# Partial sums of two middle chunks moved from one addition to a copy and an addition, with one weight buffer fewer

## The chip, the core and the metric

The kernel runs on one core of one Trainium2 chip. The core's engines are TensorE (PE: matmuls; PEld is its weight loads), VectorE (DVE), ScalarE (ACT), GpSimd (POOL) and SyncE (SP), which here only issues transfers (DMA). Each engine works through its own queue in order; semaphores tie the queues together. SBUF is the working memory, 128 partitions wide; PSUM is the memory that matmuls write to, eight banks of 128 x 512 float32. The metric is the time of one execution in microseconds, the median of the runs shown.

## What is computed

The reference is one layer of an encoder block over 256 tokens of width 2048. What the change touches is its first product, the combined input projection of the normalised and modulated tokens:

```python
mod = cond @ w_ada[l] + b_ada[l]
shift1, scale1, gate1, shift2, scale2, gate2 = jnp.split(mod, N_ADA, axis=-1)
h = modulate(rms_norm(x, norm_mix[l]), shift1, scale1)
proj = h @ w_in[l]
qa, ka, va, qi, ki, wi, qb, fb, ib, gb, g_a, g_b = split_columns(proj, IN_WIDTHS)
...
x = x + gate1[:, None, :] * (mixed @ w_out[l])
```

Behind it come an attention over selected keys, a gated recurrence, an output projection and a retrieval over 16384 experts. All products are float32, done as three products each: a matrix is split into a high part and a low rest, and high times high, high times low and low times high are added.

## The kernel before

**Phase 1, the projection sets.** 6144 of the projection's columns are computed in the loop `for c, ks in enumerate(CHUNKS)` as three sets `s` of 2048 columns, of which each fills the eight PSUM banks (16 column blocks of 256 tokens). The 16 k-tiles of 128 input features come in four chunks of 2, 3, 5 and 6. For each chunk and set, TensorE goes over the chunk's k-tiles, 48 matmuls each (a step; 48 steps in all), and adds them up in the eight banks. Then the banks are emptied into SBUF, and the next set uses them. In the first chunk the banks are copied, in turn by ScalarE and VectorE (L455, L457). In the three later chunks VectorE adds each bank to what is in SBUF (`nc.vector.tensor_add(d, d, p)`, L459). `into` tells the places: `dsa`, `qk`, `qkr`, `sgb`. In the first and the second set one bank goes to two places, so there are 26 pieces in a chunk: 22 of 128 x 512 and 4 of 128 x 256.

**The h1 tiles.** The k-tiles of h are made while the loop runs. `h1_tile(n)` needs two sums over 2048 products of the conditioning vector with a row of `w_ada` (VectorE, `ada_dot`, L186, tile `ada`), then GpSimd multiplies a tile of x by the root mean square (L240), ScalarE makes its high part (L242) and VectorE the modulated tile and the low part (L243, L244).

**The weights.** Class `Feed` loads weights in units of 128 x 1024 (512 KB), two for a step. `raw` (L76) issues a transfer on SP into the next of the `raw` buffers, which are used in turn: three of pool `raws` and two of pool `more`. `_split` makes the high part `hi` on ScalarE (L90) and the low part `lo` on VectorE, or on GpSimd for every third unit (L94, `pool_every = 3`, during phase 1's first part). There are three `hi` and three `lo` buffers; up to two units are split ahead. A `raw` buffer is free again when its `lo` is done. `ada_rest` takes `raw` buffers in the same turn for the other rows of `w_ada`, which one VectorE product consumes (L186, tile `raw`).

**Where the pools end.** `more` lives until the whole first phase ends (L874): sets, attention, recurrence, the gates, the projections `w_up`, and `w_out`. After that the feed has the three buffers of `raws` alone.

**Order.** The engines' queues are laid out by a scheduler when the program is built; `pin` keeps some instructions in the order of the program. The loop that empties the banks stands in the program behind the matmuls of its set.

Of the kernel before, what the change touches and what calls it, by code (L numbers as in the profile page):

```python
# [8 lines left out]
F32 = mybir.dt.float32  # L9
# [5 lines left out]
AF = mybir.ActivationFunctionType  # L15
# [5 lines left out]
P = 128  # L21
# [83 lines left out]
def build(tc, a):  # L105
    nc = tc.nc
    root = ExitStack()
    const = root.enter_context(tc.tile_pool(name="const", bufs=1))
    raws = root.enter_context(tc.tile_pool(name="raws", bufs=3))
# [6 lines left out]
    def bank(name="bank"):  # L116
        return psum.tile([P, 512], F32, tag="bank", name=name)
# [4 lines left out]
    feed = Feed(nc, [raws], his, los, ahead=2)  # L122
# [14 lines left out]

    p1 = ExitStack()
    k16 = p1.enter_context(tc.tile_pool(name="k16", bufs=7))
    more = p1.enter_context(tc.tile_pool(name="more", bufs=2))  # L140
    feed.raw_pools = [raws, more, raws, more, raws]

    def big(dt=F32, name="big"):
        return k16.tile([P, 4096], dt, tag="k16", name=name)

    ctx1 = ExitStack()


    small = ctx1.enter_context(tc.tile_pool(name="small", bufs=1))
# [14 lines left out]
    def ada_load(g):  # L164
        t = big(name="ada").rearrange("p (s k) -> p s k", s=2)
        for sec in range(2):
            tc.keep_in_program_order(nc.sync.dma_start(t[:, sec, :], a["w_ada1"][g, sec]))
        ada_tiles[g] = t

    feed.pin = tc.keep_in_program_order  # L170
    CHUNKS = (range(0, 2), range(2, 5), range(5, 10), range(10, 16))
# [254 lines left out]
    for c, ks in enumerate(CHUNKS):  # L426
        for s in range(3):
            banks = [bank(f"set{s}_{b}") for b in range(8)]
            for k in ks:
                if step in loads:  # L430
                    ada_load(loads[step])
                if feed.todo:
                    feed.load()
                    feed.load()
                if step == 40:
                    feed.pin = None
                units = [feed.next(), feed.next()]
                if step in makes:
                    h1_tile(makes[step])
                for b in range(16):  # L440
                    whi, wlo = units[b // 8]
                    out = banks[b // 2][:, (b % 2) * T:(b % 2 + 1) * T]
                    i = products(out, whi, wlo, (b % 8) * 128, hh[:, k, :], hl[:, k, :],
                                 k == ks[0] and b % 2 == 0, k == ks[-1],
                                 after=prev if k == ks[0] and b % 2 == 1 else None)
                    prev = i
                step += 1
                if c == len(CHUNKS) - 1 and step >= 36:
                    ada_bg.run(1700)
            for i, (ps, dst) in enumerate(zip(banks, into[s])):  # L450
                parts = [(dst, ps)] if not isinstance(dst, tuple) else [
                    (d, ps[:, z * T:(z + 1) * T]) for z, d in enumerate(dst)]
                for d, p in parts:
                    if c == 0 and i % 2:
                        nc.vector.tensor_copy(d, p)  # L455
                    elif c == 0:
                        nc.scalar.activation(d, p, AF.Copy)  # L457
                    else:
                        nc.vector.tensor_add(d, d, p)  # L459

# [105 lines left out]
    for c in range(2):  # L566
        ps = s_block(hh, hl, *W_A)
# [191 lines left out]
    for c in range(2):  # L759
        ps = s_block(hh, hl, *W_A)  # L760
# [793 lines left out]
```

## Time and profile before

| | us |
|---|---|
| median of 3 runs | 2158.49 |
| lowest and highest run | 2154.59, 2158.61 |
| the profiled execution | 2151.07 |
| its span, first to last instruction | 2149.2 |

| engine | busy, us | share of the span |
|---|---|---|
| PE | 2035.7 | 95% |
| PEld | 1841.5 | 86% |
| DVE | 1644.7 | 77% |
| ACT | 1068.9 | 50% |
| POOL | 1025.7 | 48% |

The first matmul of the sets starts at 29 us, the last ends at 355 us; the four chunks begin at about 29, 74.4, 141.2 and 237.8 us. Busy time is an average over stages; a stage is read by its own stretch, and by the waits that end last in it. A wait stands as "who waits <- for whom".

### The profile page before, as it was taken

How to read it: one execution, taken by the hardware profiler on the slowest of the kernel's cores; microseconds unless marked ns; L12 is line 12 of the kernel's file. 1: busy time of each engine (PE TensorE's matmuls, PEld its weight loads, DVE VectorE, ACT ScalarE, POOL GpSimd, SP SyncE). 2: the span in 40 equal slices, each digit the busy share in tenths (PEclk: the TensorE clock that was granted, in tenths of full speed). 3: DMA queues.
4: the chain of work that ended last, by engine and by line, in shares of the span. 5: the costliest groups of instructions: out<-in, count | busy, mean ns of one | idle time of the engine just before them, and what ended most of it. 6: DMA issues, size and time to landing. Idle time of an engine off the chain costs nothing. (4 is left out here: it accounts for less than half of the span.)

```text
span 2149.2 us, 34359 instructions
## 1 busy us (share of the span) xinstructions
PE 2035.7 (95%) x12916; PEld 1841.5 (86%) x12916; DVE 1644.7 (77%) x2538; ACT 1068.9 (50%) x1559; POOL 1025.7 (48%) x663
## 2 busy tenths in 40 slices
PE   6989999999999999999999999998999989999996
PEld 6988998779999999899888888887888778886885
DVE  7899888878675888887999666687558776765687
ACT  3433334455645445444666555543554445654575
POOL 3333422224420001218777688777871026777763
PEclk8999999999999999999999999999999999999998
DMA  6878778676677899857777898899879979999994
GB/s 252 310 267 317 258 254 288 207 239 210 214 236 263 312 334 326 310 176 183 180 181 186 231 262 257 249 324 291 223 212 360 319 261 334 282 261 268 386 382 178
DMA packets 208832, 568.65 MB, mean 265 GB/s; under 512 B 57585, under 2 KB 89489, under 8 KB 191633
## 3 DMA queue, kind: packets, MB, share of 16 engines
q1 hardware_dynamic: 147248, 441.38, 59.5%
q0 software_dynamic: 58928, 123.94, 21.5%
q8 instruction: 103, 1.69, 0.3%
q10 hardware_dynamic: 2482, 1.07, 0.2%
q14 instruction: 71, 0.58, 0.1%
HBM read 544.95 MB, written 38.06 MB: 271 GB/s over the span
## 5 line engine op out<-in xcount | busy, mean ns | idle before, releaser
L90 ACT ACTIVATE hi<-raw 128x1024 fp32r<-128x1024 f32 x550 | 580.9, 1058 | 686.0 <-PE ps_w L120 270.6
L94 DVE TENSOR_TENSOR lo<-raw,hi 128x1024 fp32r<-128x1024 f32 x506 | 652.5, 1292 | 256.0 <-ACT hi L90 254.3
L120 PE MATMUL ps_w<-h,hi 128*128 128x512 f32 (+1 forms) x2560 | 811.9, 373 | 12.7 <-ACT hi L90 7.4
L120 PE MATMUL ps_w<-h,lo 128*128 128x256 f32 x2304 | 649.5, 282 | 10.5 <-DVE lo L94 10.5
L921 POOL DMA_INDIRECT gtab<-gate,addr x256 | 508.7, 1987 | 174.9 <-issue 70.9
L120 PEld LDWEIGHTS ps_w<-h,hi 128*128 128x128 f32 x2560 | 465.0, 189 | 100.1 <-ACT hi L90 9.2
L120 PEld LDWEIGHTS ps_w<-h,lo 128*128 128x128 f32 x2304 | 437.0, 190 | 17.4 <-DVE lo L94 16.6
L120 PE MATMUL out<-vh,ap 128*128 128x512 f32 x1008 | 313.3, 391 | 2.8 <-ACT vh L225 2.8
L226 DVE TENSOR_TENSOR vl<-v,vh 128x1024 fp32r<-128x1024 f32 x190 | 224.6, 1224 | 72.7 <-ACT vh L225 70.7
L94 POOL TENSOR_TENSOR lo<-raw,hi 128x1024 fp32r<-128x1024 f32 x44 | 117.6, 2673 | 294.1 <-ACT hi L90 294.1
L120 PEld LDWEIGHTS out<-vh,ap 128*128 128x128 f32 x1008 | 189.5, 188 | 44.4 <-ACT vh L225 5.3
L225 ACT ACTIVATE vh<-v 128x1024 fp32r<-128x1024 f32 x190 | 189.8, 1047 | 72.4 <-DMA v<-w_v,index 67.7
L120 PE MATMUL set<-h1hi,hi 128*128 128x256 f32 x768 | 212.3, 291 | 13.5 <-ACT h1hi L242 7.1
L120 PE MATMUL set<-h1hi,lo 128*128 128x256 f32 x768 | 198.5, 293 | 22.1 <-DVE lo L94 18.9
L120 PE MATMUL set<-h1lo,hi 128*128 128x256 f32 x768 | 212.8, 288 | 0.9 <-DVE h1lo L244 0.9
L120 PE MATMUL out<-vl,ap 128*128 128x512 f32 x504 | 197.6, 392 | 4.9 <-DVE vl L226 4.9
L186 DVE SCALAR_TENSOR_TENSOR raw<-raw,cond 128x1024 f32<-128x1024 f32 x96 | 134.2, 1404 | 49.6 <-DMA raw<-w_ada 45.9
L120 PEld LDWEIGHTS set<-h1hi,hi 128*128 128x128 f32 x768 | 150.1, 198 | 16.6 <-ACT h1hi L242 7.3
L120 PEld LDWEIGHTS set<-h1hi,lo 128*128 128x128 f32 x768 | 141.2, 199 | 26.6 <-DVE lo L94 23.1
L120 PE MATMUL ps_w<-h1hi,hi 128*128 128x256 f32 x528 | 150.8, 286 | 3.0 <-ACT hi L90 3.0
L120 PE MATMUL ps_w<-h1hi,lo 128*128 128x256 f32 x528 | 150.3, 285 | 1.9 <-DVE lo L94 1.9
L120 PEld LDWEIGHTS set<-h1lo,hi 128*128 128x128 f32 x768 | 150.9, 197 | 1.2 <-DVE h1lo L244 1.2
(356 smaller groups left out, 3196.6 us busy)
## 6 DMA issues: line engine op xcount, KB each, us to landing
raw<-w_u SPq DMA_DIRECT2D x256, 512.0 KB, 4.4
raw<-w_sets SPq DMA_DIRECT2D x96, 512.0 KB, 5.4
raw<-w_ada SPq DMA_DIRECT2D x96, 512.0 KB, 5.1
raw<-w_t SPq DMA_DIRECT2D x66, 512.0 KB, 4.6
ada<-w_ada SPq DMA_DIRECT2D x32, 1024.0 KB, 8.3
raw<-w_s SPq DMA_DIRECT2D x32, 512.0 KB, 4.6
gtab<-zeros_d SPq DMA_DIRECT2D x32, 512.0 KB, 5.5
raw<-w_up SPq DMA_DIRECT2D x32, 512.0 KB, 4.7
```

Of the source, the lines that this page charges most:

```text
L90: self.nc.scalar.activation(hi, raw, AF.Copy)
L94: i = eng.tensor_sub(lo, raw, hi.bitcast(F32))
L120: return nc.tensor.matmul(out, lhsT, rhs, start=start, stop=stop, skip_group_check=True)
L186: return nc.vector.scalar_tensor_tensor(w, w, 1.0, cond[:, k0:k0 + n], op0=ALU.mult, op1=ALU.mult, accum_out=col)
L225: nc.scalar.activation(hi, v, AF.Copy)
L226: (lo_eng or nc.vector).tensor_sub(lo, v, hi.bitcast(F32))
L921: return nc.gpsimd.indirect_dma_start(out=gtab[tt].rearrange("p (x o) -> (p x) o", o=1), out_offset=bass.IndirectOffsetOnAxis(ap=addr[:, t ...
```

## The change

In the second and the third chunk a bank is no longer added to SBUF by VectorE in one instruction. ScalarE copies the bank into a tile `part`, and GpSimd adds `part` to the place in SBUF. There are two `part` buffers of 128 x 512 (2 KB of a partition each), in a pool that lives as long as the other small tiles of phase 1. Their 4 KB are those of one `raw` buffer: pool `more` has one instead of two, and the feed turns through four buffers instead of five. First and last chunk are emptied as before.

```diff
     p1 = ExitStack()
     k16 = p1.enter_context(tc.tile_pool(name="k16", bufs=7))
-    more = p1.enter_context(tc.tile_pool(name="more", bufs=2))
-    feed.raw_pools = [raws, more, raws, more, raws]
+    more = p1.enter_context(tc.tile_pool(name="more", bufs=1))
+    feed.raw_pools = [raws, more, raws, raws]
...
     ctx1 = ExitStack()
+    parts = ctx1.enter_context(tc.tile_pool(name="parts", bufs=2))
...
             for i, (ps, dst) in enumerate(zip(banks, into[s])):
-                parts = [(dst, ps)] if not isinstance(dst, tuple) else [
+                pieces = [(dst, ps)] if not isinstance(dst, tuple) else [
                     (d, ps[:, z * T:(z + 1) * T]) for z, d in enumerate(dst)]
-                for d, p in parts:
+                for d, p in pieces:
                     if c == 0 and i % 2:
                         nc.vector.tensor_copy(d, p)
                     elif c == 0:
                         nc.scalar.activation(d, p, AF.Copy)
+                    elif c < len(CHUNKS) - 1:
+                        part = parts.tile([P, 512], F32, name="part")[:, 0:p.shape[1]]
+                        nc.scalar.activation(part, p, AF.Copy)
+                        nc.gpsimd.tensor_add(d, d, part)
                     else:
                         nc.vector.tensor_add(d, d, p)
```

The lines of the changed kernel have numbers one higher from here on, and five higher below the loop: L90 and L94 stay, L186 is L187, L240 is L241, L242 to L244 are L243 to L245; the copies are L461, the additions L462.

GpSimd's queue in the second chunk, before: low parts of weights (`lo`, L94) and tiles of x (L240) alone.

```order
L240 TENSOR_TENSOR x<-x,rs 128x256
L94 TENSOR_TENSOR lo<-raw,hi 128x1024 x2
L240 TENSOR_TENSOR x<-x,rs 128x256
L94 TENSOR_TENSOR lo<-raw,hi 128x1024 x2
L240 TENSOR_TENSOR x<-x,rs 128x256
```

The same place of the changed kernel, from the end of that chunk's first set on:

```order
L462 TENSOR_TENSOR dsa<-dsa,part 128x512 x4
L462 TENSOR_TENSOR qk<-qk,part 128x512 x2
L94 TENSOR_TENSOR lo<-raw,hi 128x1024
L241 TENSOR_TENSOR x<-x,rs 128x256
L462 TENSOR_TENSOR qk<-qk,part 128x512
L462 TENSOR_TENSOR qk<-qk,part 128x256
L462 TENSOR_TENSOR dsa<-dsa,part 128x256
L462 TENSOR_TENSOR qk<-qk,part 128x512 x3
L94 TENSOR_TENSOR lo<-raw,hi 128x1024
```

Six additions now stand ahead of a `lo` and a tile of x, and three or four more before the next set's.

ScalarE's queue at the same set's end, before: high parts of weights (`hi`, L90) and of h1 (L242).

```order
L90 ACTIVATE hi<-raw 128x1024 x5
L242 ACTIVATE h1hi<-x,mod 128x256
L90 ACTIVATE hi<-raw 128x1024 x3
L242 ACTIVATE h1hi<-x,mod 128x256
L90 ACTIVATE hi<-raw 128x1024 x4
```

And in the changed kernel, where `set_3_665` is bank 3 of the set that ends and `set_0_888` bank 0 of the next:

```order
L461 ACTIVATE part<-set_3_665 128x512
L90 ACTIVATE hi<-raw 128x1024
L461 ACTIVATE part<-set_4_666 128x512
L461 ACTIVATE part<-set_5_667 128x512
L90 ACTIVATE hi<-raw 128x1024
L243 ACTIVATE h1hi<-x,mod 128x256
L461 ACTIVATE part<-set_6_668 128x512
L461 ACTIVATE part<-set_7_669 128x256
L90 ACTIVATE hi<-raw 128x1024
L461 ACTIVATE part<-set_7_669 128x256
```

One or two copies, of which each waits for a free `part`, now stand ahead of each `hi`.

VectorE's queue at the end of that set, before:

```order
L459 TENSOR_TENSOR qk<-qk,set_5_664 128x512
L459 TENSOR_TENSOR qk<-qk,set_6_665 128x512
L459 TENSOR_TENSOR qk<-qk,set_7_666 128x256
L459 TENSOR_TENSOR dsa<-dsa,set_7_666 128x256
L186 SCALAR_TENSOR_TENSOR ada,dots<-ada,cond 128x2048
L235 TENSOR_SCALAR mod<-dots,bada,cols 128x1
L94 TENSOR_TENSOR lo<-raw,hi 128x1024
```

And in the changed kernel in the same chunk:

```order
L245 TENSOR_TENSOR h1lo<-x,h1hi 128x256
L94 TENSOR_TENSOR lo<-raw,hi 128x1024
L187 SCALAR_TENSOR_TENSOR ada,dots<-ada,cond 128x2048 x2
L236 TENSOR_SCALAR mod<-dots,bada,cols 128x1
L94 TENSOR_TENSOR lo<-raw,hi 128x1024
L238 TENSOR_SCALAR mod<-dots,bada 128x1
```

The additions are gone; `lo` and the `ada` products stand next to each other, the two products of a tile in a row.

## Rows read from the trace of the kernel before

**Rows 1.** Busy time by stretch; columns in the first line.
```profile
core 0: us, PE busy (x) PEld busy (x) DVE busy (x) ACT busy (x) POOL busy (x), PEclk, DMA share, GB/s
74.40:141.20 66.80, 57.45 (x435) 56.02 (x434) 62.89 (x71) 21.70 (x23) 25.07 (x11) 0.92 0.74 278
141.20:237.80 96.60, 88.52 (x723) 86.83 (x722) 92.07 (x92) 35.08 (x36) 39.28 (x16) 1.00 0.78 290
...
690.00:903.00 213.00, 210.40 (x1751) 209.81 (x1750) 179.06 (x254) 96.83 (x128) 15.94 (x13) 1.00 0.90 319
```

**Rows 2.** PE's waits, 74.4 to 237.8 us: total us, times, longest.
```profile
PE set L120 <- DVE lo L94: 12.8, 9, 3.5
PE set L120 <- DVE qk L459: 3.6, 3, 1.8
```

**Rows 3.** Groups, 74.4 to 237.8 us: count, busy us, mean ns, idle before.
```profile
L186 DVE SCALAR_TENSOR_TENSOR ada<-ada,cond 128x2048 f32<-128x2048 f32 x22 | 62.3, 2832 | 0.0
L94 DVE TENSOR_TENSOR lo<-raw,hi 128x1024 fp32r<-128x1024 f32 x32 | 54.6, 1707 | 2.7 <-ACT hi L90 2.7
L90 ACT ACTIVATE hi<-raw 128x1024 fp32r<-128x1024 f32 x48 | 50.8, 1059 | 81.6 <-PE set L120 76.2 <-issue 5.4
L94 POOL TENSOR_TENSOR lo<-raw,hi 128x1024 fp32r<-128x1024 f32 x16 | 46.2, 2887 | 97.3 <-ACT hi L90 97.3
L240 POOL TENSOR_TENSOR x<-x,rs 128x256 f32<-128x256 f32 x11 | 19.4, 1762 | 0.0
```

**Rows 4.** Line 459, whole span: duration ns min/median/max, first and last start.
```profile
L459 DVE TENSOR_TENSOR qk<-qk,set x27: 405/674/689, 96.5 to 319.3; 128x512 f32<-128x512 f32 x21, 128x256 f32<-128x256 f32 x6
```

**Rows 5.** VectorE's timeline, 91 to 114 us: start us, us, instruction.
```profile
97.08 1.21 DVE L94 TENSOR_TENSOR lo<-raw,hi 128x1024 fp32r<-128x1024 f32 x1
...
107.61 2.28 DVE L186 SCALAR_TENSOR_TENSOR ada<-ada,cond 128x2048 f32<-128x2048 f32 x1
...
110.16 3.42 DVE L94 TENSOR_TENSOR lo<-raw,hi 128x1024 fp32r<-128x1024 f32 x1
```

**Rows 6.** GpSimd's timeline, 91 to 170 us.
```profile
109.81 2.69 POOL L94 TENSOR_TENSOR lo<-raw,hi 128x1024 fp32r<-128x1024 f32 x1 [3.53 <-ACT hi L90]
...
166.18 2.40 POOL L94 TENSOR_TENSOR lo<-raw,hi 128x1024 fp32r<-128x1024 f32 x1 [8.59 <-ACT hi L90]
168.53 0.74 POOL L240 TENSOR_TENSOR x<-x,rs 128x256 f32<-128x256 f32 x1
```

**Rows 7.** GpSimd's timeline, 505 to 516 us, in the recurrence.
```profile
508.42 1.30 POOL L678 TENSOR_TENSOR zt<-zt,qkr 128x512 f32<-128x512 f32 x1 [1.51 <-ACT zt L674]
509.68 1.31 POOL L679 TENSOR_TENSOR zt<-zt,qkr 128x512 f32<-128x512 f32 x1
510.94 2.28 POOL L681 TENSOR_TENSOR zt<-zt,qkr 128x512 f32<-128x512 f32 x1
```

**Rows 8.** Busy time and granted clock, two stretches; columns as in the first group.
```profile
130.00:135.00 5.00, 1.46 (x13) 1.25 (x11) 5.00 (x7) 0.48 (x1) 3.22 (x2) 0.84 0.85 354
133.00:140.00 7.00, 5.09 (x24) 5.09 (x25) 6.75 (x11) 1.66 (x2) 0.78 (x1) 0.53 0.74 236
```

**Rows 9.** Line 76's loads, 279 to 346 us: count, issue ns; time to landing.
```profile
L76 SPq DMA_DIRECT2D raw<-w_sets x20: 327/328/441, 279.8 to 336.6; - x20
L76 SPq DMA_DIRECT2D raw<-w_ada x17: 327/328/387, 279.5 to 344.9; - x17
...
DMA to landing us min/median/max: 3.7/5.4/7.1
```

**Rows 10.** Line 76's loads, 803 to 886 us.
```profile
L76 SPq DMA_DIRECT2D raw<-w_out x29: 327/328/328, 804.5 to 886.0; - x29
L76 SPq DMA_DIRECT2D raw<-w_ada x23: 327/328/328, 803.1 to 884.3; - x23
...
DMA to landing us min/median/max: 3.8/5.0/6.1
```

**Rows 11.** SP's waits, 803 to 886 us: total us, times, longest.
```profile
SPq L76 <- DVE lo L94: 34.4, 25, 2.4
```

## The prediction

> **What bounds the kernel now.** I first read the stretches of the page's timeline by chunk. The second and third chunk of k-tiles run from 74.4 to 237.8 us, 163.4 us. TensorE issues 24 steps of 48 matmuls there, 1152 in all; where nothing holds it, it starts 1751 in 213 us, 0.1216 us each [rows 1], so 140 us would do and some 23 us are lost. The PE waits say to whom: VectorE's `lo` 12.8 us, VectorE's additions out of PSUM 3.6 us [rows 2]. VectorE is busy 155 of the 163.4 us, ScalarE 57, GpSimd 64 [rows 1]. So VectorE bounds this stretch, and the change takes work from it: at first sight a gain of up to 23 us.
>
> The question is why VectorE is so full. In the groups of instructions its `ada` products take 2832 ns in the mean where one undisturbed takes 2.28 us, and its `lo` 1707 ns where one takes 1.21 [rows 3, 5]. The timeline of the two engines shows why: GpSimd's `lo` runs from 109.81 to 112.50, and VectorE's `lo`, begun at 110.16, takes 3.42 us, that is the rest of GpSimd's instruction and then its own 1.2 [rows 5, 6]. An operation with two SBUF inputs on one engine and one on the other exclude each other. The additions from PSUM are different: the 27 into qk, over the whole stage, lie between 405 and 689 ns (the three other destinations, 51 more, alike) [rows 4]. They never waited. The change takes away the VectorE work that runs beside GpSimd, and gives GpSimd work that doesn't run beside VectorE.
>
> The Trainium skill, page "SBUF — State Buffer", section "Who interferes with whom", says the same as a rule: a VectorE instruction with two SBUF inputs contends with a GpSimd instruction that reads SBUF, one with at most one SBUF input does not, and the loser blocks for the whole instruction. The trace agrees, 3.42 against 1.21 us. Taken at its word, no microsecond of the new additions hides behind VectorE's two-input work, which is the upper account below.
>
> **The change part by part.** *Removed:* two chunks times 26 additions (seven or eight banks whole, one or none in two halves, three sets): 44 at 0.674 and 8 at 0.405 us [rows 4] = 32.9 us of VectorE; five of the six evictions begin inside the stretch, 27.4 us.
>
> *Added on ScalarE:* 52 copies. A copy of 512 columns takes no longer than the 1.06 us of a `hi` with its 1024 [rows 3], so at most 55 us on an engine idle for 106 us of this stretch [rows 1]: nothing in busy time. But each copy needs one of two `part` buffers, so the third copy of a set waits for GpSimd's first addition, and behind it in ScalarE's queue stand the `hi` of the next k-tiles.
>
> *Added on GpSimd:* 52 additions with two SBUF inputs. The nearest rows are GpSimd's 128x512 products of the later recurrence: 508.42 to 509.68, 1.26 us a piece alone, 2.28 when VectorE is in between [rows 7]; a half piece is 0.74 [rows 6]. 44 x 1.26 + 8 x 0.74 = 61.4 us; five evictions are 51.
>
> Now the shared resource. Before, its holders in the stretch were 22 `ada` products x 2.28 = 50, 32 VectorE `lo` x 1.21 = 39, 16 GpSimd `lo` x 2.40 = 38, 11 products `x` x 0.74 = 8 [rows 3, 5, 6]: 135 of 163.4 us. With 51 more it is 186. So if it never idled the stretch would last 23 us longer; that is the lower end. From VectorE's side: before, it was held up 22 x 0.55 + 32 x 0.50 = 28 us by 46 us of GpSimd, the rest of GpSimd's time lay behind the additions and small operations that don't collide. With those gone nearly all of GpSimd's time is met by a waiting VectorE: 51 + 18 - 27 = 42 us longer, the upper end. I take 32, the middle, and 3 us for the sixth eviction, which delays the first set of the last chunk: **+35**.
>
> *Clock:* after TensorE had been busy for only 1.46 of the 5 us from 130 to 135, its granted clock was 0.53 in 133 to 140, mostly the lower of the two levels (1.2 GHz) [rows 8]. The new stalls at set ends should bring one such dip that counts: **+2** (0 to +6).
>
> *One weight buffer fewer*, over all of phase 1, not only here. In 279 to 346 us 37 loads are issued, 1.81 us each, and land after 5.4 us [rows 9]; five buffers turn round in 9.05 us, of which 3.65 are not flight. With four buffers at the same turn it is 2.26 a load, +17 us over 37; if the flight falls to the 3.7 of the quickest, 7.35 / 4 = 1.84, +1. I take **+9**. From 690 to 903 us TensorE is full (210.4 of 213 us busy) and DMA at 0.90 [rows 1]. In 803 to 886, 52 loads, 1.60 us each, median flight 5.0, quickest 3.8 [rows 10]; SP waited 34.4 us there for VectorE's `lo` alone to free a buffer [rows 11]: each load goes out as its buffer is released. The turn is 7.98 us. Use alone (`hi` 1.06 plus `lo` 1.21 for a weight [rows 3, 5]; for a row of the conditioning one product over as many columns, I take the 1.21 of a `lo`) is (29 x 2.27 + 23 x 1.21) / 52 = 1.8 us, so about 1.2 us is slack that can go. Four buffers: (5.0 + 1.8) / 4 = 1.70 a load, +6%, 13 us over 213; with part of the slack staying 17; with the 3.8 of the quickest 1.40, nothing. Flight shortens a little with fewer under way: **+10** (0 to +17). From 355 to 690 the cover is TensorE's own pace at a DMA load the page shows as lower; I cost it at nothing, +3 if that cover is gone.
>
> The Trainium skill, same page, section on the DMA setup-cost knee, gives a transfer about 2 us plus its bytes at 436 GB/s; for 512 KB that is an estimate of 3.2 us. By it the four buffers would turn in time and the two buffer terms were 0, the time 19 us lower. The landings in both stretches, 5.4 and 5.0 us with several loads under way, speak against it.
>
> Sum: 35 + 2 + 9 + 10 = 56 us. The profiled execution took 2151.07 us (span 2149.2 and 1.9 around it): 2207. The median of the runs shown, 2158.49, is 7.4 above that execution: 2158.5 + 56 = **2214 us**.
>
> **The rivals.**
> A, *faster*: the additions find the shared port free. VectorE loses 27.4 us, TensorE can win back at most 23; with buffers hidden by TensorE's pace some -18: 2140. It decides at 27 us: if less than 27 of the 51 + 18 us that can collide do, VectorE gains. For it: TensorE's stalls leave VectorE idle at set ends, just when the additions come. Against: 135 of 163 us are held already. Chance 0.06.
> B, *no change*: only the share of GpSimd's time that collides today (28 of 46, 0.6) collides: 51 x 0.6 - 27.4 = +3, buffers hidden: 2161. Chance 0.06.
> C, *banks come free too late*: eight banks leave through two `part` buffers. An addition alternating with a VectorE operation takes 1.26 + about 1.7 = 3 us; the last whole bank waits for six of them and one `lo`, 20 us after the first is complete, where TensorE is back at that bank after some 10. 10 us by six set ends are 60 instead of 35: 2240. For it: the order has `lo` and `x` in between; against: while TensorE stands, VectorE runs dry and additions go at 1.26. Chance 0.15.
> D, *the buffer is the larger part*: the turn does not shrink, +17 in the last chunk and +17 or more later, with 37: 2158 + 71 and up, 2230 to 2255. Chance 0.12.
> E, *only the floor*: +23 for the port, flight shortens, no buffer term: 2182. Chance 0.11.
> That the change does not do what it says is excluded by the order: all 52 copies and additions stand there.
>
> **How the numbers follow.** The forecast (2195 to 2230) has 0.50. The range reaches from just under E to C and most of D, 2174 to 2252; A and B, 0.12, and the tail of D are left out. A measurement of this kernel tells 0.2%, 4 us, from no change. Faster is A, 0.06; same is B, 0.06; slower is the rest, 0.88.
>
> **What would show it.** Right: the stretch of the two middle chunks grows from 163 to some 195 us; VectorE's mean `lo` and `ada` product grow although it has 52 instructions fewer; GpSimd's additions take 1.3 to 3.5 us, with a mean about 2; PE's waits name `lo`, and copies on ScalarE wait for GpSimd; from 690 us on, ScalarE's waits for landing weights and PE's idle time grow. Wrong: middle chunks at or under 163 us (the lock matters little), additions at 1.3 us throughout with VectorE's means unchanged, or a last chunk and output projection at their old length (the fifth buffer was spare).

## The result, and the profile after

The changed kernel takes 2223.07 us (median of 6 runs, 2212.16 to 2229.55) against 2158.55 us before (6 runs beside them, 2151.48 to 2163.12): ratio 1.029, 95% interval 1.0262 to 1.0317, slower by some 64.5 us (difference of the medians). The forecast was 2214, its range 2174 to 2252. The profiled execution took 2229.16 us, span 2227.4.

The time by stretch. A stretch begins at TensorE's first matmul of it. Both kernels were profiled twice (the second executions are two of the runs below), because one execution alone turns out to be a poor measure of some stretches. The last column is what the prediction put there.

| stretch of before | before, two executions | after, two executions | forecast |
|---|---|---|---|
| up to 74.4, first chunk | 74.4, 74.3 | 75.4, 75.6 | 0 |
| to 237.8, the two middle chunks | 163.4, 161.0 | 180.9, 183.0 | +34 (port 32, clock 2) |
| to 354.8, last chunk | 117.0, 113.4 | 128.0, 126.7 | +12 (buffer 9, sixth eviction 3) |
| to 414.7 | 59.9, 63.5 | 63.5, 60.2 | 0 |
| to 606.5, up to the attention's output | 191.8, 191.1 | 199.2, 203.8 | 0 |
| to 690.7 | 84.2, 84.2 | 84.3, 84.2 | 0 |
| to 903.3, output projection and mixing | 212.6, 213.9 | 236.2, 236.1 | +10 |
| to 1763.1 | 859.8, 871.5 | 871.0, 877.5 | 0 |
| to the end | 386.1, 386.2 | 388.9, 402.7 | 0 |

So four stretches grew, by some 17 to 22, 10 to 15, 7 to 13 and 23 us. Of those the first two are those of the projection sets; the other two have nothing of the new eviction in them, only the fourth weight buffer. The stretch to 1763 us differs by 12 us between two executions of the kernel before, so what it shows of one execution of after is no effect of the change. Nor is the 402.7 us of the last stretch: the eight kernels below that were profiled on one chip, this execution of after among them, all take 399 to 406 us there, the other six executions 384 to 389.

Busy time of after in the four stretches (us, then each engine's busy time and instructions, granted clock of TensorE, DMA share, GB/s); the first answers to [rows 1], the last to its third row:

```profile
75.40:256.30 180.90, 154.50 (x1154) 149.85 (x1153) 156.04 (x117) 78.84 (x105) 154.54 (x72) 0.92 0.68 256
256.30:384.30 128.00, 113.26 (x867) 109.79 (x865) 87.24 (x100) 44.91 (x47) 40.28 (x21) 0.95 0.71 240
447.80:647.00 199.20, 184.46 (x1308) 172.62 (x1307) 145.59 (x206) 110.44 (x160) 62.12 (x38) 0.97 0.63 215
731.30:967.50 236.20, 220.05 (x1751) 213.28 (x1751) 179.55 (x254) 95.87 (x128) 16.25 (x13) 0.99 0.86 287
```

In the first row three things are to be seen beside [rows 1]. VectorE is busy for 156.0 us, against 155.0 before, with 45 instructions fewer: nearly all of the 27 us that were taken from it came back as longer instructions. GpSimd went from 64 to 154.5 us. And TensorE was idle for 26.4 us (180.9 - 154.5), against 17.4 (163.4 - 146.0), and took 8.5 us more for the same 1152 matmuls, at a granted clock of 0.92 against 0.97. The stretch's 17.5 us are thus 9 us of waits and 8.5 us of clock.

The groups of instructions of after in the middle chunks (count, busy us, mean ns, idle before), which answer to [rows 3]:

```profile
L187 DVE SCALAR_TENSOR_TENSOR ada<-ada,cond 128x2048 f32<-128x2048 f32 x22 | 76.2, 3481 | 6.4 <-DMA ada<-w_ada 6.4
L94 DVE TENSOR_TENSOR lo<-raw,hi 128x1024 fp32r<-128x1024 f32 x32 | 55.8, 1742 | 15.3 <-ACT hi L90 14.4 <-issue 0.9
L245 DVE TENSOR_TENSOR h1lo<-x,h1hi 128x256 fp32r<-128x256 f32 x10 | 14.4, 1444 | 0.3
L244 DVE TENSOR_SCALAR x<-x,mod 128x256 f32<-128x256 f32 x10 | 10.4, 1036 | 3.2 <-ACT h1hi L243 3.1
L94 POOL TENSOR_TENSOR lo<-raw,hi 128x1024 fp32r<-128x1024 f32 x15 | 45.8, 3054 | 20.8 <-ACT hi L90 20.8
L462 POOL TENSOR_TENSOR qk<-qk,part 128x512 f32<-128x512 f32 (+1 forms) x18 | 30.8, 1731 | 1.3 <-ACT part L461 1.3
L462 POOL TENSOR_TENSOR qkr<-qkr,part 128x512 f32<-128x512 f32 x13 | 28.9, 2244 | 3.2 <-ACT part L461 3.2
L461 ACT ACTIVATE part<-set 128x512 f32<-128x512 f32 (+1 forms) x47 | 26.1, 559 | 50.8 <-POOL qkr L462 18.2 <-POOL dsa L462 14.7 <-POOL qk L462 11.0
L462 POOL TENSOR_TENSOR dsa<-dsa,part 128x512 f32<-128x512 f32 (+1 forms) x10 | 24.7, 2496 | 1.0 <-ACT part L461 1.0
```

VectorE's `ada` product went from 2832 to 3481 ns and the two short steps of an h1 tile from 847 to 1444 (`h1lo`) and from 695 to 1036 ns (L244); `lo`, whose mean the prediction saw growing too, hardly changed, from 1707 to 1742. GpSimd's 46 additions (with the five into `sgb`, 9.4 us, not shown) take 93.8 us, 2.04 us each; ScalarE's copies are short, 0.56 us, and wait 43.9 us for GpSimd's additions to give a `part` buffer back. What TensorE waited for in the middle chunks (total us, times, longest), answering to [rows 2]:

```profile
PE set L120 <- ACT part L461: 13.0, 9, 2.7
PE set L120 <- ACT hi L90: 4.7, 2, 3.8
PE set L120 <- POOL lo L94: 3.3, 3, 1.7
PE set L120 <- DVE lo L94: 3.3, 2, 2.6
```

In the second execution the wait for copies is 17.6 us. Before, 12.8 us were VectorE's `lo`. Now the largest is a bank that ScalarE hasn't copied out yet, because GpSimd hasn't added the copy before the last.

### The profile page after: what moved, and what is told of

Its sections match the earlier page's. It is cut to its first block, busy times and chain, and to the rows that moved or that the text cites. A ratio compares the mean times of both kernels' runs of the same rounds, so it can differ in the third digit from the quotient of the medians.

```text
span 2227.4 us, 34468 instructions
## 1 busy us (share of the span) xinstructions
PE 2069.6 (93%) x12916; PEld 1860.2 (84%) x12916; DVE 1649.7 (74%) x2486; ACT 1094.3 (49%) x1611; POOL 1137.1 (51%) x715
## 3 DMA queue, kind: packets, MB, share of 16 engines
q0 software_dynamic: 58928, 123.94, 20.8%
## 5 line engine op out<-in xcount | busy, mean ns | idle before, releaser
L90 ACT ACTIVATE hi<-raw 128x1024 fp32r<-128x1024 f32 x550 | 580.5, 1058 | 697.5 <-PE ps_w L120 224.3
L94 DVE TENSOR_TENSOR lo<-raw,hi 128x1024 fp32r<-128x1024 f32 x506 | 660.6, 1308 | 314.1 <-ACT hi L90 308.1
L926 POOL DMA_INDIRECT gtab<-gate,addr x256 | 525.9, 2054 | 170.3 <-issue 70.4
L120 PE MATMUL set<-h1hi,hi 128*128 128x256 f32 x768 | 219.6, 300 | 36.8 <-ACT part L461 15.3
L94 POOL TENSOR_TENSOR lo<-raw,hi 128x1024 fp32r<-128x1024 f32 x44 | 116.6, 2650 | 223.8 <-ACT hi L90 209.2
L120 PE MATMUL set<-h1hi,lo 128*128 128x256 f32 x768 | 190.9, 297 | 11.2 <-DVE lo L94 7.7
L120 PEld LDWEIGHTS set<-h1hi,hi 128*128 128x128 f32 x768 | 155.7, 205 | 43.6 <-ACT part L461 17.9
L187 DVE SCALAR_TENSOR_TENSOR raw<-raw,cond 128x1024 f32<-128x1024 f32 x96 | 134.8, 1407 | 53.1 <-DMA raw<-w_ada 43.0
L120 PEld LDWEIGHTS set<-h1lo,hi 128*128 128x128 f32 x768 | 156.1, 204 | 3.4 <-DVE h1lo L245 3.4
```

The source lines that it names most:

```text
L90: self.nc.scalar.activation(hi, raw, AF.Copy)
L94: i = eng.tensor_sub(lo, raw, hi.bitcast(F32))
L120: return nc.tensor.matmul(out, lhsT, rhs, start=start, stop=stop, skip_group_check=True)
L187: return nc.vector.scalar_tensor_tensor(w, w, 1.0, cond[:, k0:k0 + n], op0=ALU.mult, op1=ALU.mult, accum_out=col)
L926: return nc.gpsimd.indirect_dma_start(out=gtab[tt].rearrange("p (x o) -> (p x) o", o=1), out_offset=bass.IndirectOffsetOnAxis(ap=addr[:, t ...
```

## The experiments

Each ratio is to the kernel before, run on the same chip beside it; its median there was 2172.70, 2176.75 or 2156.23 us, so kernels are set against each other by their ratios, which are taken from the single runs and not from the medians. A difference in us that is read from ratios is that share of 2158 us. The queues of each kernel are laid out anew when it is built, so an edit also shifts other instructions: the eviction with five buffers has five additions in a row on GpSimd where after has six.

### Is it the shared port? `lo` without GpSimd

If GpSimd's operations block VectorE's, the opposite of the change should pay: the kernel before with the 44 `lo` of GpSimd given to VectorE, the busiest engine of the middle chunks.

```diff
-    feed.pool_every = 3
+    feed.pool_every = 0
```

> The kernel before with every low part of the sets' and the following weights (44 of them) on VectorE and none on GpSimd. In the middle chunks VectorE gets 16 more of 1.21 us, 19 us, on an engine busy for 155 of 163 us. Lock theory: it was held up 28 us there by GpSimd's two-input work, and what is left of that (11 products x of 0.74 us) holds it up at most 8, so VectorE needs 155 - 20 + 19 = 154 us or a little less waiting for low parts: 163 to 155 us, and in the first and last chunk the like; 2145 to 2156 for all. Theory of plain load (an engine's queue is as long as its own work, GpSimd only helps): the middle chunks grow by up to 19 us, first and last chunk by 5 to 10 each, about 2185. VectorE's mean low part falls from 1707 ns to under 1350 by the lock theory and stays by the other.

Measured: 2144.6 us, ratio 0.9866 (0.9807 to 0.9924); and, repeated later,

> The kernel before with all of lo on VectorE in the projections, in more rounds beside the next: ratio to before 0.985 to 0.988.

2136.53 us, 0.9901 (0.9872 to 0.993), a little above what was expected. Its middle chunks (first execution), by the groups and the second execution's stretches:

```profile
L94 DVE TENSOR_TENSOR lo<-raw,hi 128x1024 fp32r<-128x1024 f32 x48 | 58.5, 1228 | 4.5 <-ACT hi L90 4.5
L186 DVE SCALAR_TENSOR_TENSOR ada<-ada,cond 128x2048 f32<-128x2048 f32 x22 | 50.3, 2295 | 4.9 <-DMA ada<-w_ada 4.9
```

```profile
0.00:77.90 77.90, 57.18 (x385) 55.30 (x386) 58.41 (x72) 29.99 (x38) 30.48 (x28) 0.85 0.74 277
77.90:228.50 150.60, 142.51 (x1155) 139.21 (x1154) 140.15 (x182) 56.58 (x59) 0.00 (x0) 1.00 0.83 308
```

VectorE does 16 `lo` more and is busy for less, 140 against 155 us, because each `lo` takes 1228 ns in place of 1707 and each `ada` 2295 in place of 2832. The middle chunks fall from 163.4 to 150.4 us. Of VectorE's 155 us before, 22 x 0.54 + 32 x 0.48 = 27 us were thus waiting inside instructions for GpSimd. That settles that VectorE is held up by GpSimd's work; and since its instructions grew longer again in after, the additions didn't find the port free, as rival A had it.

### The change's two parts, each alone

*The fourth buffer alone*, on the kernel before:

```diff
-    more = p1.enter_context(tc.tile_pool(name="more", bufs=2))
-    feed.raw_pools = [raws, more, raws, more, raws]
+    more = p1.enter_context(tc.tile_pool(name="more", bufs=1))
+    feed.raw_pools = [raws, more, raws, raws]
```

> The kernel before with four raw buffers instead of five, its additions left on VectorE. The trace of the change has 163.4 us between the starts of the second and the fourth chunk turned to 180.9 (+17.5), the last chunk 117.0 to 128.0 (+11), from there to the first product with att 251.7 to 262.7 (+11), att to rec as before, and from the first product with rec to the end of the output projection 212.6 to 236.2 (+24). Theory 1 (the buffer is the larger part, the move of the additions the smaller): middle chunks as before (within 4 us), and +9, +11, +24 in the three later stretches: 2158 + 44, about 2202. Theory 2 (the delays of the middle chunks and the other order of the queues carry on, and the buffer is hidden by the pace of TensorE): all stretches within 3 us of before, about 2160.

Measured: 2204.51 us, ratio 1.0126 (1.0076 to 1.0176), that is 27 us. Its stretches:

```profile
73.00:230.00 157.00, 141.91 (x1155) 139.03 (x1153) 149.54 (x162) 57.12 (x59) 64.28 (x27) 1.00 0.80 299
230.00:347.80 117.80, 107.78 (x867) 104.51 (x865) 87.60 (x108) 41.48 (x41) 30.15 (x13) 1.00 0.76 258
411.60:611.30 199.70, 185.52 (x1310) 172.90 (x1308) 146.83 (x206) 110.54 (x160) 64.00 (x38) 0.97 0.64 215
695.50:931.70 236.20, 219.79 (x1752) 213.22 (x1751) 180.84 (x254) 96.44 (x128) 16.33 (x13) 0.99 0.86 289
```

The last two are those of after to the microsecond (199.2 and 236.2), so what after lost in these two is the buffer's: 8 and 23.6 us. In the last chunk the buffer costs next to nothing alone (117.8 against 117.0 and 113.4).

*The new eviction alone*, with five buffers; the two part buffers lie in columns of `dsa` that are free at that time:

```diff
-    more = p1.enter_context(tc.tile_pool(name="more", bufs=1))
-    feed.raw_pools = [raws, more, raws, raws]
+    more = p1.enter_context(tc.tile_pool(name="more", bufs=2))
+    feed.raw_pools = [raws, more, raws, more, raws]
...
-                        part = parts.tile([P, 512], F32, name="part")[:, 0:p.shape[1]]
+                        turn = (turn + 1) % 2
+                        part = dsa[:, 2560 + 512 * turn:2560 + 512 * turn + p.shape[1]]
```

> The changed kernel with five raw buffers; the two part buffers are columns 2560 to 3583 of tile dsa, which nothing uses before the sets are done. So only the path of the partial sums is changed. Theory 1: middle chunks +15 to +18, the first set of the last chunk +3, everything behind as before: 2158 + 20, about 2178. Theory 2: the later stretches stay as slow as in the change, about 2215. If the price of the middle chunks too came from the buffer: 2158 within 4.

Measured: 2196.39 us, ratio 1.0103 (1.0062 to 1.0144), that is 22 us:

```profile
73.30:256.60 183.30, 154.06 (x1154) 148.95 (x1152) 152.99 (x120) 78.52 (x106) 154.23 (x73) 0.93 0.68 253
256.60:366.10 109.50, 106.84 (x865) 106.43 (x866) 83.92 (x95) 44.86 (x47) 49.38 (x22) 0.97 0.80 277
704.60:918.10 213.50, 210.25 (x1747) 209.49 (x1746) 177.61 (x254) 96.98 (x128) 17.49 (x13) 1.00 0.90 318
```

The middle chunks are as long as in after, so they are the eviction's alone; the stretch behind is as before. The last chunk is 18 us shorter than in after and shorter than before. So in the last chunk neither part costs anything alone that one execution, with its scatter of 3.6 us there, could show.

*The whole change once more*, beside other kernels of this section:

> The changed kernel itself once more, beside the three others on one chip, so that its parts can be added up on the same footing. The fourth buffer alone gave 1.0126 and the split eviction with five buffers 1.0103 of before; if the two only add, this is 1.023; if the last chunk's interaction of 10 to 18 us is in the kernel and not in one profiled execution, it is 1.028 to 1.031, and the last chunk takes 125 us or more again.

Measured: 2242.69 us, ratio 1.0306 (1.0244 to 1.0369). 1.0126 and 1.0103 add up to 1.023; the 0.008 that are missing, 17 us, are no more than the three intervals together leave open (about 0.009), so the ratios don't show that the parts cost more together. The stretches do: the last chunk takes 126.7 us here too, against 117.8 and 109.5 with one part alone.

### Are the banks short of part buffers?

This is the rival "banks come free too late", with four part buffers in place of two (its last two in `dsa`):

```diff
-                        part = parts.tile([P, 512], F32, name="part")[:, 0:p.shape[1]]
+                        slot = (slot + 1) % 4
+                        part = (parts.tile([P, 512], F32, name="part")[:, 0:p.shape[1]] if slot % 2 else
+                                dsa[:, 2560 + 256 * slot:2560 + 256 * slot + p.shape[1]])
```

> The changed kernel (four raw buffers) with four part buffers instead of two: the two of the pool and two in columns of tile dsa that nothing uses at that time. In the trace of the change PE waited 13.0 us in the middle chunks for copies of ScalarE, and these 44 us for GpSimd's additions. Theory of the banks: with four buffers half of the banks are copied before the first addition is done, PE's wait for copies falls to under 4 us and the middle chunks from 181 to about 170: 2223 - 11, about 2212. Lock theory: the additions still take 2 us each because VectorE's two-input work is in between, ScalarE waits later instead, and the middle chunks stay within 5 us of 181: 2218 to 2224.

Measured: 2250.02 us, ratio 1.0326 (1.0272 to 1.038); middle chunks 192.5 us, 10 longer than with two. TensorE's waits in them:

```profile
PE set L120 <- POOL lo L94: 14.6, 4, 6.0
PE set L120 <- DVE lo L94: 12.9, 9, 2.6
PE set L120 <- ACT dsa L463: 3.6, 2, 2.5
```

The wait for the copies went, as the rival had it (3.6 us, and 2.2 for its other two buffers, against 13.0), and came back larger for `lo`. With more buffers the queues are laid out with more additions in a row on GpSimd: eight, five and five ahead of the first three `lo` behind the first eviction, where two buffers have six, six and three. A `lo` in the same queue waits behind all of them: the one that ends TensorE's longest wait, 6.0 us, begins at 137.8 us, behind five additions that fill GpSimd from 127.4 us on. The two part buffers kept `lo` from waiting.

### What do the additions cost?

The changed kernel without line 462: ScalarE copies, and nobody adds.

```diff
                         nc.scalar.activation(part, p, AF.Copy)
-                        nc.gpsimd.tensor_add(d, d, part)
```

> The changed kernel without GpSimd's additions: the middle chunks' banks are copied by ScalarE and the copies are dropped, so the second and third chunk's partial sums are left out of the result. This prices the additions by themselves; ScalarE's copies, VectorE's relief and the fourth buffer stay. Theory, GpSimd is what the middle chunks wait for (its 46 additions of about 2 us hold both VectorE's port and the copies): middle chunks 145 to 154 us in place of 181 to 183, the last chunk 112 to 120 in place of 127 to 128, the stages behind unchanged with the fourth buffer's 31 us; ratio to before 1.005 to 1.013 in place of 1.031. Rival, ScalarE's copies (28 us between the high parts of the weights) make the matmuls wait by themselves: middle chunks 160 us or more, ratio 1.015 or more.

Measured: 2176.76 us, ratio 1.0101 (1.0056 to 1.0145):

```profile
74.30:220.70 146.40, 140.87 (x1155) 139.94 (x1153) 120.41 (x120) 77.25 (x109) 60.54 (x27) 0.99 0.83 319
220.70:338.40 117.70, 108.92 (x864) 106.04 (x864) 81.11 (x96) 43.23 (x44) 30.71 (x14) 0.98 0.74 259
```

The copies as such disturb nobody: TensorE is busy for 140.9 of 146.4 us at a clock of 0.99. The additions cost 34.5 to 36.6 us in the middle chunks (180.9 and 183.0 against 146.4), for 46 of them. The change's 17 to 22 us is the difference between that and the 15 to 17 us that VectorE's relief brings, copies and clock included (163.4 and 161.0 to 146.4). The last chunk falls from 127 or 128 to 117.7 with four buffers kept: its extra length comes from the additions too, though in after the last of them ends 17 us into it (at 273.8 us).

### Lock or queue? The change without `lo` on GpSimd

Two costs of the additions can still be told apart: that they block VectorE, and that GpSimd's `lo`, which the matmuls need, stands behind them. The split eviction with five buffers and all `lo` on VectorE has the first alone:

```diff
-    feed.pool_every = 3
+    feed.pool_every = 0
```

> The split eviction with five raw buffers (the parts lie in columns 2560 to 3583 of the tile dsa), and all of lo on VectorE, so that GpSimd has only the additions and the products of x with rs, and nothing that the matmuls wait for queues behind an addition but the eviction itself. The kernel with lo on VectorE and the old eviction took 150.4 us for the middle chunks, of which VectorE was busy 140.1. Theory of the shared port: VectorE gives away some 52 additions of 0.63 (33 us), but GpSimd's 52 additions hold the port 1.26 us each (66 us), and VectorE's lo and ada get longer by about that; middle chunks 155 to 173 us, VectorE's mean lo above 1500 ns and its ada above 2800, whole kernel 5 to 20 us above the kernel with lo on VectorE (ratio to before 0.989 to 0.997). Rival, engine load alone: VectorE has 33 us less to do, lo and ada keep their 1228 and 2295 ns, middle chunks at or under 150 us, whole kernel at or under the ratio 0.987.

Measured: 2178.46 us, ratio 1.002 (0.9981 to 1.0059), some 33 us above the kernel with `lo` on VectorE and the old eviction by its first ratio (0.9866), 26 by its second (0.9901), beyond the 20 that the port theory gave. Groups and waits of the middle chunks, 171.2 us:

```profile
L94 DVE TENSOR_TENSOR lo<-raw,hi 128x1024 fp32r<-128x1024 f32 x47 | 70.5, 1515 | 25.0 <-ACT hi L90 24.8
L186 DVE SCALAR_TENSOR_TENSOR ada<-ada,cond 128x2048 f32<-128x2048 f32 x22 | 59.2, 2710 | 0.8 <-DMA ada<-w_ada 0.8
```

```profile
PE set L120 <- ACT dsa L461: 17.2, 13, 2.3
PE set L120 <- DVE lo L94: 2.5, 1, 2.5
```

VectorE's `lo` goes from 1228 to 1515 ns and its `ada` from 2295 to 2710, 47 x 0.29 + 22 x 0.42 = 23 us, with nothing on GpSimd but the additions and a few products of `x`: the lock takes back most of the 29 us that VectorE was relieved of (47 additions from PSUM, 28.7 us by the groups of that kernel), and VectorE is busy for no less, 143.7 against 140.1 us. The 20.8 us that the stretch is longer are 12 us more of TensorE's idle time, now 17.2 us for copies and 2.5 for `lo`, and 9 us of clock (0.93 against 1.00). So the eviction through two engines gives VectorE no relief, and it is the longer way for a bank to come free.

The same with the changed kernel's four buffers:

> The changed kernel (four raw buffers, split eviction) with all of lo on VectorE. This tells apart where the last chunk's 11 us came from, which neither the fourth buffer alone (+1) nor the split eviction with five buffers (-8) has. Theory 1, the last set's additions stand ahead of GpSimd's lo as the last chunk begins, PE starves and its clock falls: without lo on GpSimd the last chunk takes 110 to 118 us. Theory 2, VectorE is late when the last chunk begins and four buffers don't bridge it: the last chunk takes 122 us or more. The middle chunks by the shared port: 155 to 175 us (181 in the changed kernel). Whole kernel: ratio to before 1.003 to 1.010 by theory 1 (the 31 us of the buffer in the stages behind stay), 1.008 to 1.018 by theory 2.

Measured: 2205.2 us, ratio 1.0152 (1.009 to 1.0215); the last chunk 116.4 us, which is theory 1's, and the whole within theory 2's range, since theory 1's sum had the stretches behind too low (204.0 and 237.0 us there). Moving `lo` off GpSimd takes 10 to 12 us from the last chunk (126.7 and 128.0 to 116.4). With five buffers it was 107.5 us, so 9 us of the fourth buffer stay even then.

The trace of after shows where the last chunk loses. Stretches of 5 us at its beginning and in its third part, and GpSimd's timeline at the beginning (start us, us, instruction):

```profile
255.00:260.00 5.00, 2.74 (x22) 2.33 (x20) 2.58 (x5) 3.27 (x6) 5.00 (x3) 1.00 0.32 116
260.00:265.00 5.00, 2.93 (x13) 2.73 (x14) 4.96 (x3) 1.94 (x3) 5.00 (x4) 0.69 0.46 141
265.00:270.00 5.00, 5.00 (x30) 5.00 (x29) 2.39 (x2) 2.03 (x3) 3.13 (x2) 0.63 0.95 344
...
310.00:315.00 5.00, 1.28 (x9) 1.07 (x8) 1.93 (x3) 1.57 (x2) 1.78 (x1) 0.81 0.77 270
315.00:320.00 5.00, 5.00 (x26) 5.00 (x26) 4.05 (x6) 0.68 (x2) 0.00 (x0) 0.51 0.80 253
```

```profile
254.53 4.55 POOL L462 TENSOR_TENSOR qkr<-qkr,part 128x512 f32<-128x512 f32 x2
259.04 2.35 POOL L94 TENSOR_TENSOR lo<-raw,hi 128x1024 fp32r<-128x1024 f32 x1
```

As the last chunk begins, GpSimd does the middle chunks' last additions, with its `lo` between them; TensorE has little to do for some 4 us and then runs at a mean granted clock of 0.63 to 0.69, so for most of that time at the lower of its two levels (1.2 and 2.4 GHz). Around 312 us it starves a second time, for weights that come late (ScalarE stands 4.5 and 3.9 us before the two `hi` at 308.3 and 313.2 us until their units land), and goes on at 0.51, almost wholly at the lower level. The second execution of after has both stalls, and only the first with a fall of the clock:

```profile
260.00:265.00 5.00, 2.41 (x9) 2.06 (x10) 4.82 (x4) 2.03 (x3) 5.00 (x3) 0.67 0.00 0
265.00:270.00 5.00, 5.00 (x31) 5.00 (x30) 3.00 (x2) 2.63 (x4) 5.00 (x4) 0.64 0.97 351
...
310.00:315.00 5.00, 2.32 (x20) 2.11 (x19) 4.31 (x3) 1.79 (x3) 2.36 (x1) 1.00 0.76 279
```

The first is the additions'. Waits for `hi` come with four buffers in any case: with four buffers alone TensorE waits 5.2 us for it in the last chunk's sets and 3.3 us at its end, in the kernel before not at all; but 6.3 us of waits for `lo` go away there, and the stretch is no longer. Why they go away was not tried further.

### A version that beats both

The kernel before with `lo` on VectorE, and GpSimd's last work in the projections, the product of `x` and `rs`, fused into VectorE's step:

```diff
-        for m in (0, 1) if n == 0 else (n + 1,):
-            if m < KT:
-                pin(nc.gpsimd.tensor_mul(x[:, m, :], x[:, m, :], rs))
         h = x[:, n, :]
-        nc.scalar.activation(hh[:, n, :], h, AF.Identity, bias=mod[:, 0, n:n + 1], scale=mod[:, 1, n:n + 1])
-        pin(nc.vector.tensor_scalar(h, h, mod[:, 1, n:n + 1], mod[:, 0, n:n + 1], op0=ALU.mult, op1=ALU.add))
-        pin(nc.vector.tensor_sub(hl[:, n, :], h, hh[:, n, :].bitcast(F32)))
+        pin(nc.vector.scalar_tensor_tensor(h, h, mod[:, 1, n:n + 1], rs, op0=ALU.mult, op1=ALU.mult))
+        nc.scalar.activation(hh[:, n, :], h, AF.Identity, bias=mod[:, 0, n:n + 1])
+        pin(nc.vector.scalar_tensor_tensor(hl[:, n, :], h, mod[:, 0, n:n + 1], hh[:, n, :].bitcast(F32),
+                                           op0=ALU.add, op1=ALU.subtract))
...
-    feed.pool_every = 3
+    feed.pool_every = 0
```

> The kernel before with lo on VectorE in the projections, and the product of x with rs fused into VectorE's step ahead of the split of h1 (t = x * mod1 * rs in one instruction; ScalarE adds mod0 and makes the high part; one instruction of VectorE subtracts it), so that GpSimd has no work on tiles in the projections at all. Theory of the shared port: the last of VectorE's lengthened instructions go, and ScalarE's high part of h1 waits no more for GpSimd's x (9.9 us of waits in the first 78 us); 3 to 8 us under the kernel with lo on VectorE alone: ratio to before 0.983 to 0.985. Rival: what is left in the first chunk is set by the loads of ada's weights and by the chain dots, mod, h1, whose length the fusion doesn't change: ratio 0.986 to 0.988.

Measured: 2143.73 us, ratio 0.9863 (0.9805 to 0.992), no different from the kernel with `lo` on VectorE alone, though its projections ended 11 us earlier in the trace. So both were run once more, in more rounds:

> The same with the product of x and rs fused into VectorE's step. Its projections ended 11 us earlier in the trace, and its time was the same within the spread. If the gain of the projections reaches the end, its ratio is 0.004 to 0.005 below the other's (0.981 to 0.983); if a later stretch gives it back, the two are within 0.001.

Measured: 2129.36 us, ratio 0.9858 (0.9825 to 0.989), beside 0.9901 (0.9872 to 0.993) of the other: 7 us less. The intervals overlap, so the difference is likely, not certain; that both are faster than the kernel before, by 1 to 1.5%, is clear of both intervals. Its stretches, beside the two rows of the other shown above:

```profile
0.00:64.80 64.80, 53.99 (x384) 52.42 (x385) 51.93 (x72) 29.18 (x38) 5.91 (x12) 0.92 0.85 329
64.80:214.70 149.90, 142.24 (x1154) 139.22 (x1153) 142.00 (x184) 55.56 (x59) 0.00 (x0) 1.00 0.82 311
```

The gain is in the first chunk, 64.8 against 77.9 us. The middle chunks don't change.

### How far one execution bears

> The kernel before once more, for the lengths of its stretches in a second execution: chunks of 67, 97 and 117 us, middle chunks 160 to 165, the stretch from the recurrence's weights to the end of the mixing 213 us. Differences of over 3 us in a stretch between the two executions bound what a single comparison of stretches can bear; the fourth buffer alone showed 157 us in the middle chunks, and if the second execution of before shows 157 to 160 too, that gain is none.

Measured: 2160.86 us in its one run, with the stretches of the table at the top; three of them:

```profile
74.30:235.30 161.00, 143.58 (x1154) 140.47 (x1153) 154.43 (x162) 56.79 (x59) 63.96 (x27) 0.99 0.77 289
235.30:348.70 113.40, 106.51 (x867) 104.42 (x866) 88.92 (x107) 41.51 (x41) 32.70 (x15) 1.00 0.77 266
...
901.40:1772.90 871.50, 839.01 (x4955) 737.23 (x4953) 646.42 (x1234) 439.27 (x745) 544.22 (x308) 0.98 0.83 239
```

Stretches of the projections repeat to within 2 to 4 us, that from 691 to 903 to 1.3, and that of the experts only to 12. The 157.0 us that four buffers alone showed in the middle chunks is 4 us under this, too little to call a gain.

## Why the prediction was right, and which of its steps were not

**What bounds the kernel before: right.** VectorE's instructions were long because of GpSimd; with nothing beside them, `lo` and `ada` take 1228 and 2295 ns, the 1.21 and 2.28 us that the prediction read from single rows. The Trainium skill, page "SBUF — State Buffer", section "Who interferes with whom", has this as a rule, and for the instructions that the prediction counts the runs agree on who blocks whom. The same section excepts VectorE's 2-port modes from what it says of instructions with at most one SBUF input; the prediction left that out, and after has such a case: L244, with one tensor in SBUF, takes 0.40 us at 176.56, where GpSimd is idle, and 1.16 us at 158.57, where a GpSimd addition runs until 159.58. Whether it runs in such a mode no run shows. Another of its pages would have pointed the other way: "Perfetto Trace Analysis", section "Identifying the Most-Contended Engine", calls the occupancy of VectorE a fair measure of how close one is to the limit, and has the most occupied engine optimized first. Here 27 of VectorE's 155 busy us, in `lo` and `ada` alone, were waiting for a lock, and giving it more work made the kernel faster; the measurement decides.

**The port, +35 (32 in the middle chunks): direction right, size too large, and the wait misnamed.** Measured are 17 to 22 us there, clock included, below even the lower end of 23. By the prediction's durations the holders in after sum to 50 + 39 + 36 + 8 + 54 = 187 us, and the stretch is 180.9. The sum is too high because the records of neighbouring instructions overlap: in the kernel with `lo` on VectorE its 182 instructions of the middle chunks sum to 154.6 us by their groups and keep it busy for 140.1, 0.08 us less each; by that an estimated 10 us of the 187 are counted twice. The account itself, a port that is never free, is what after shows: counted from the trace's records, an `ada`, `lo` or `h1lo` of VectorE or an instruction of GpSimd is under way in 176 of the 180.9 us, before in 132 of 163.4. The upper end's account was nearer to the truth than its price: VectorE's relief was indeed eaten (155.0 to 156.0 us busy), but VectorE no longer sets the end. TensorE waits for copies, 13.0 us, and for `lo` of either engine only 6.6 (17.6 and 7.7 in the second execution); the prediction said that its waits would go on naming `lo`. That is the mechanism of rival C, "banks come free too late", at a smaller price than its 60 us, and without its remedy: four part buffers made it worse. Priced by themselves, the additions cost 35 to 37 us and the relief is worth 15 to 17.

**Clock, +2 (0 to +6): too small.** TensorE's busy time for the same matmuls rose by 8.5 us in the middle chunks and by 4 to 7 in the last. The forecast had one dip that counts; looked at in pieces of 5 us the stretch has five, at 105, 115 to 125, 140, 155 to 165 and 225 to 235 us. Four follow waits for copied banks of 2.3 to 2.7 us; the deepest, 0.81 and then 0.51, comes with a wait of 3.8 us for `hi`.

**Last chunk, +12: right size, wrong working.** It grew by 10 to 15 us. But the prediction added 9 us of the buffer to 3 us of the eviction, and the runs show nothing for each alone (117.8 and 109.5 us, against 117.0 and 113.4); only together do they cost, by the stalls above and their clock. The account of how often five buffers turn round priced the loads. With the new eviction and no `lo` on GpSimd the buffer does cost 9 us (107.5 to 116.4); with VectorE's additions its waits for `hi` only take the place of waits for `lo`. That the forecast's two terms add up to the measured size is luck.

**The buffer behind 414 us: too small in both places.** From 355 to 690 us I put 0, or 3 if TensorE's own pace were no cover; measured 7 to 13, 8 with the buffer alone. In after ScalarE waits 22.2 us for `dsa` of VectorE there, 11.3 before, and VectorE is busy for 5.7 us more: its `lo` take 1467 ns in the mean, 1381 before, and its products of loaded rows 1622, 1349 before. Why they grow with a buffer fewer is open. From 690 to 903 I put 10 (0 to 17); measured 23.6 with the buffer alone and 22 to 24 in after. The loads of its second half (issues of line 76; time to landing), answering to [rows 10], and ScalarE's largest wait there (8.6 us before):

```profile
L76 SPq DMA_DIRECT2D raw<-w_out x30: 327/328/328, 859.0 to 954.5; - x30
L76 SPq DMA_DIRECT2D raw<-w_ada x25: 327/328/328, 860.5 to 960.4; - x25
L76 SPq DMA_DIRECT2D raw<-w_q x4: 327/328/328, 958.1 to 965.7; - x4
...
DMA to landing us min/median/max: 3.5/4.9/6.5
```

```profile
ACT hi L90 <- DMA raw<-w_out: 45.7, 24, 5.1
```

59 loads in 108.7 us are 1.84 us each, a turn of four in 7.37 us, of which 4.9 are flight and 2.5 are not. The forecast had 6.8: the flight right (4.9 against 5.0 there; in the first half of the stretch 4.7 against 5.1, so it did shorten a little, as the forecast said), but 1.8 us for the use, counted from durations alone. 0.7 us of waiting between landing, `hi` and `lo`, and release, which I had called slack that can go, stayed, on each of them: 0.17 us a load. The time per load rose by 10% (in 809.3 to 903.3 us of before 56 loads took 1.68 us each), not 6.

**The other rivals.** "No change" and "the port is free" fell with the first experiment. "Only the floor" had the port's price nearly right, and the port was as good as never free; it left the buffer out. "The buffer is the larger part" had the size of the stretches from 690 us nearly right; of the whole, the buffer is 27 us and the eviction 22 alone; some 15 us, by the last chunk's stretches, come only with both together.

**Sum.** Port and clock were 12 to 17 us too high, the buffer behind 414 us some 22 too low, the last chunk right. The 2214 us came out 9 below the result because two errors nearly cancel, not because each term was good.

## What to carry to other kernels

Before work is moved off a busy engine, subtract from its busy time what it spends blocked: compare the mean of each kind of instruction with its quickest, undisturbed row. If VectorE is blocked by GpSimd's two-input operations, take work from GpSimd, even where VectorE is the busier, as it was here. Price a buffer by removing that buffer alone: a turn counted from durations leaves out the small waits between landing and release, and two changes that are free alone may not be free together. When an eviction goes through another engine's queue, look at what else stands in that queue; more buffers can make it worse, since more of that work is then laid out ahead of what others wait for.

## What the runs showed of the hardware that was not expected

The additions from PSUM on VectorE and ScalarE's copies from PSUM are about as quick, 0.67 and 0.60 us for 512 columns, and neither is disturbed by GpSimd: none takes over 0.69 and 0.60 us. The same additions on GpSimd take 2.04 us in the mean beside a working VectorE. An instruction of VectorE with one tensor in SBUF (L244) was held up by GpSimd as well, 0.40 to 1.16 us and more. The records of neighbouring instructions overlap, so sums of durations come out too high, by 14.5 us of 154.6 in one stretch. Landing got little quicker with four loads under way in place of five (medians of 4.7 and 4.9 against 5.1 and 5.0 us in the two halves of the stretch from 690 us). And the same kernel needs 12 us more or less in the experts' stretch from one execution to the next, with 826.7 or 839.0 us of TensorE's busy time at 0.99 or 0.98 of its clock, and the last stretch of all took 399 to 406 us in the eight executions on one chip and 384 to 389 in the six others, whatever the kernel.
